# A decoder trunk in split float32: down projections of two ConvFFN parts from seven block products instead of eight

## The chip, the cores and the metric

The kernel runs on one core of a Trainium2 chip. The metric is the device time of one execution in microseconds. The time before is the median of three runs.

## The reference, cut to what matters

The trunk has two layers on 512 tokens with 1024 channels. Layer 0 mixes tokens with dilated attention, layer 1 with a Mamba-2 scan; each mixer is followed by a gated ConvFFN, and a last RMSNorm ends the trunk. The change is in the ConvFFN:

```python
def conv_ffn(h, w_up, conv_w, conv_b, w_down):
    u = causal_depthwise_conv(h @ w_up, conv_w, conv_b)
    gate, up = u[..., :D_FF], u[..., D_FF:]
    return (jax.nn.silu(gate) * up) @ w_down
...
for i in range(DEPTH):
    ...
    h = rmsnorm(x, ffn_norm_w[i])
    x = x + conv_ffn(h, ffn_w_up[i], ffn_conv_w[i], ffn_conv_b[i], ffn_w_down[i])
return rmsnorm(x, final_norm_w)
```

`D_FF` is 2816 and the convolution has three taps. All of it is float32.

## The kernel before, in words

**Layout.** Activations lie transposed: channels on the 128 partitions, the 512 tokens along the free axis. The residual stream is eight tiles `xr[0..7]` of 128x512. The normalised input of a projection is kept as eight pairs of tiles, `xh[k]` and `xl[k]`: a rounded high part and the remainder, both in the 4-byte type float32r.

**Split products.** A float32 product is built from three products of such parts: `mm3` (L136) issues high weights by high data, high weights by low data, low weights by high data, all added up in one PSUM bank. Each goes through `long_product` (L133 to L134), so nearly all of TensorE's matmuls carry line 134. One matmul has 128 rows of contraction, 128 output channels and 512 tokens.

**Weights.** `load_unit` (L116) fetches a block of 128x1024 float32 weights by one DMA on SyncE's queue into a tile `raw` (a ring of 4 buffers, `wr`), rounds it to `hi` on ScalarE (L125) and puts the remainder into `lo` on VectorE (L126). `hi` and `lo` have rings of 5 buffers each (`wh`), so the weights of at most five units exist at a time.

**ConvFFN.** `ffn` (L610) works through the 22 blocks of hidden channels in three parts of 8, 8 and 6 blocks (`FF_PARTS`). For each block `c` there are two up projections, gate and up (units `2c` and `2c+1`), each of 8 x 3 matmuls (`project`, L146) into a bank of the ring `mm` (3 banks). VectorE scales the bank by the row norms `rbc` into an SBUF tile `us` (L620), which frees the bank. `conv` then makes tile `a` from `us`: ScalarE applies the last tap and the bias (L603), VectorE adds the two other taps (L605). ScalarE applies Silu (L624), GpSimd multiplies gate and up (L627), ScalarE rounds the result to `g_h` (L629) and GpSimd makes `g_l` (L630). Then the part's down projection follows: `down` (L263) runs over the eight output blocks `m`, with one weight unit of up to 128x1024 each and 3 matmuls for each hidden block, and VectorE adds the finished bank to `xr[m]` (L640). In a part of 8 hidden blocks that is 8 x 8 x 3 = 192 matmuls. The last part of layer 1 goes through `finish` (L1059), which computes the last two output blocks in halves of 256 tokens: its matmuls have 256 columns, its residual adds (L1076) 256 too.

**Other buffers.** PSUM has three rings: `mm` with 3 banks, `aux` with 3 and `side` with 2. In SBUF, the ring `a` has 13 tiles of 128x512, `us` 3, `high` and `low` 8 each (the split activations of one part), `tmp` and `sq` 2 each. Tiles `xdt`, `yt`, `lm`, `ee` and `prev` belong to the scan of layer 1.

**Order.** A planner orders each engine's instructions by a simulated time line when the kernel is built. Where the code opens `manual_schedule` for TensorE, as around `down`, TensorE's order is that of the code, while VectorE, ScalarE and GpSimd are still ordered by the planner. The engines execute their queues strictly in order, and SyncE's queue issues the DMAs of weights.

## Time and profile before

| what | value |
|---|---|
| median of three runs | 1626.72 us (1626.13 to 1626.76) |
| the profiled execution's own time | 1626.55 us |
| its span, first to last instruction | 1624.6 us |
| mean granted TensorE clock | 0.999 |
| matmuls of one part of 8 hidden blocks | 192, at 588.2 to 630.4 us for the first |
| such parts | four: parts 0 and 1 of both layers |

In the profile, PE is TensorE's matmuls, PEld its weight loads, DVE VectorE, ACT ScalarE, POOL GpSimd and SP SyncE. A row of grouped instructions gives the line, the engine, the operation, the tiles written and read, the shapes and the count; then the busy time in us and the mean length of one in ns; then how long the engine stood idle just before, and what ended that. Matmuls are pipelined: a recorded length of 380 ns is not what one costs in a row of them, which is read from the distance between starts. The tiles of the down projections are named `wd` (and `wz` in `finish`), those of the up projections `u`.

### The profile page before, as it was taken

What the parts mean: (1) busy time and instruction counts of PE and PEld (TensorE: products, weight loads), DVE (VectorE), ACT (ScalarE), POOL (GpSimd) and SP (SyncE); (2) the same over time, 40 slices, a digit from 0 to 9 for tenths busy, and PEclk for the clock granted to TensorE, in tenths of its full rate; (3) what the DMA queues carried; (4) which work ended last, traced back from release to release, by engine and by line L of the source; (5) the groups of instructions that cost most, each with busy time, mean ns of one, the idle gap of its engine ahead of it and who ended that gap; (6) DMA issues with size and microseconds to landing.
All of it is one profiled execution on the core that took longest, in us unless ns stands there. A gap on an engine that the chain in (4) does not pass through costs nothing.

```text
span 1624.6 us, 21067 instructions
## 1 busy us (share of the span) xinstructions
PE 1615.7 (99%) x8038; PEld 1382.9 (85%) x8038; DVE 1082.8 (67%) x1813; ACT 655.0 (40%) x965; POOL 418.6 (26%) x272
## 2 busy tenths in 40 slices
PE   9999999999999999999999999999999999999998
PEld 8888888888888888888887888888888888888887
DVE  6366665266647855764657899988897784574564
ACT  5233332333334532432445455544443442342343
POOL 0444453045402320220231222222111341121020
PEclk9999999999999999999999999999999999999999
DMA  7322222222224323223233433334332232332321
GB/s 259 98 80 83 78 91 80 96 85 79 78 78 134 113 91 105 103 81 117 81 101 104 148 108 115 100 100 127 114 126 90 93 104 91 104 104 91 104 78 52
DMA packets 53235, 165.13 MB, mean 102 GB/s; under 512 B 6224, under 2 KB 9680, under 8 KB 53136
## 3 DMA queue, kind: packets, MB, share of 16 engines
q1 hardware_dynamic: 52304, 163.01, 30.5%
q8 instruction: 63, 1.03, 0.3%
q10 hardware_dynamic: 832, 0.79, 0.1%
q14 instruction: 36, 0.29, 0.1%
HBM read 161.62 MB, written 2.16 MB: 101 GB/s over the span
## 4 chain that ended last, share of the span: by engine, by line
PE 99%; ACT 0%; DVE 0%; POOL 0%; POOLq 0%; DVEq 0%; issue 0%
PE u L134 29%; PE qk L134 16%; PE wd L134 12%; PE v L134 8%; PE xs L134 5%; PE z L134 5%; PE wso L134 5%; PE wo L134 3%; PE c L134 3%; PE b L134 3%; PE wz L134 2%; PE py L830 1%; PE pg L490 1%; PE pp L477 1%; PE po L485 1%; PE pf L838 1%
## 5 line engine op out<-in xcount | busy, mean ns | idle before, releaser
L134 PE MATMUL u<-xh,lo_u 128*128 128x512 f32 x704 | 268.9, 382 | 0.0
L134 PE MATMUL u<-xh,hi_u 128*128 128x512 f32 x704 | 268.8, 382 | 0.0
L134 PE MATMUL u<-xl,hi_u 128*128 128x512 f32 x704 | 266.3, 378 | 0.0
L627 POOL TENSOR_TENSOR au<-au,au 128x512 f32<-128x512 f32 x43 | 58.5, 1360 | 422.2 <-DVE au L605 396.6
L605 DVE SCALAR_TENSOR_TENSOR au<-usu,par,au 128x511 f32<-128x511 f32 (+1 forms) x176 | 159.4, 911 | 7.6 <-ACT au L603 2.9
L125 ACT CAST hi_u<-raw_u 128x1024 fp32r<-128x1024 f32 x88 | 91.1, 1044 | 168.4 <-PE u L134 95.6
L388 POOL TENSOR_TENSOR rotqk<-rotqk,sr 32x512 f32<-32x512 f32 x48 | 88.2, 1837 | 250.2 <-DVE rotqk L387 239.8
L134 PEld LDWEIGHTS u<-xl,hi_u 128*128 128x128 f32 x704 | 131.7, 187 | 24.5
L134 PEld LDWEIGHTS u<-xh,lo_u 128*128 128x128 f32 x704 | 131.7, 187 | 24.0
L134 PEld LDWEIGHTS u<-xh,hi_u 128*128 128x128 f32 x704 | 131.7, 187 | 21.8 <-issue 0.4
L134 PE MATMUL qk<-xh,hi_qk 128*128 128x512 f32 x384 | 148.6, 387 | 0.0
L134 PE MATMUL qk<-xh,lo_qk 128*128 128x512 f32 x384 | 147.1, 383 | 0.0
L134 PE MATMUL qk<-xl,hi_qk 128*128 128x512 f32 x384 | 145.6, 379 | 0.0
L126 DVE TENSOR_TENSOR lo_u<-raw_u,hi_u 128x1024 fp32r<-128x1024 f32 x88 | 113.8, 1299 | 29.9 <-ACT hi_u L125 29.9
L620 DVE TENSOR_TENSOR usu<-u,rbc 128x512 f32<-128x512 f32 x88 | 60.3, 690 | 93.1 <-PE u L134 86.4
L640 DVE TENSOR_TENSOR xr<-xr,wd 128x512 f32<-128x512 f32 x40 | 27.3, 688 | 116.9 <-PE wd L134 116.9
L125 ACT CAST hi_qk<-raw_qk 128x1024 fp32r<-128x1024 f32 x48 | 50.3, 1047 | 130.3 <-PE qk L134 69.3
L134 PEld LDWEIGHTS qk<-xh,lo_qk 128*128 128x128 f32 x384 | 71.8, 187 | 13.3
L134 PEld LDWEIGHTS qk<-xl,hi_qk 128*128 128x128 f32 x384 | 71.9, 187 | 12.8
L389 POOL TENSOR_TENSOR qk<-qk,rotqk 32x512 f32<-32x512 f32 x48 | 81.5, 1698 | 3.8
L125 ACT CAST hi_wd<-raw_wd 128x1024 fp32r<-128x1024 f32 (+1 forms) x48 | 46.1, 972 | 88.7 <-PE wd L134 55.6
L134 PEld LDWEIGHTS qk<-xh,hi_qk 128*128 128x128 f32 x384 | 71.9, 187 | 11.2
(647 smaller groups left out, 3768.5 us busy)
## 6 DMA issues: line engine op xcount, KB each, us to landing
raw_u<-in_wup SPq DMA_DIRECT2D x88, 512.0 KB, 3.3
raw_qk<-in_wqk SPq DMA_DIRECT2D x48, 512.0 KB, 3.3
raw_wd<-in_wdn SPq DMA_DIRECT2D x32, 512.0 KB, 3.2
raw_xs<-in_win SPq DMA_DIRECT2D x16, 512.0 KB, 3.3
raw_z<-in_win SPq DMA_DIRECT2D x16, 512.0 KB, 3.4
lm<-rows SPq DMA_DIRECT2D x32, 256.0 KB, 5.4
raw_wso<-in_wso SPq DMA_DIRECT2D x16, 512.0 KB, 3.3
raw_v<-in_wv SPq DMA_DIRECT2D x12, 512.0 KB, 3.5
```

Of the source, the lines that this page charges most:

```text
L125: SC.copy(hi[:, s], raw[:, s])
L126: low.tensor_tensor(lo[:, s], raw[:, s], hi.bitcast(F32)[:, s], op=ALU.subtract)
L134: T.matmul(in_turns(dst), w, in_turns(x), start=first, stop=last)
L388: G.tensor_tensor(rot[R, :], rot[R, :], sr[R, :], op=ALU.mult)
L389: G.tensor_tensor(at(t)[R], at(t)[R], of(rot)[R], op=ALU.add)
L477: T.transpose(pp[:, b * P : (b + 1) * P], pr[:, b * P : (b + 1) * P], ident)
L485: T.matmul(po[:, ii], v0[h][:, b * P : (b + 1) * P], pts[i][:, (b - i + 1) * P : (b - i + 2) * P], start=b == max(i - 1, 0), stop=b == i,)
L490: T.matmul(pg[:, ii], vt[g, half][i][:, es], pts[i][:, (g + 1) * P : (g + 2) * P], start=g == 1, stop=g == 2,)
L605: V.scalar_tensor_tensor(dst[:, j:], src[:, : S - j], col(c_w + taps - 1 - j), dst[:, j:], op0=ALU.mult, op1=ALU.add,)
L620: V.tensor_tensor(us, p, rbc, op=ALU.mult)
L627: by.tensor_tensor(ab[1], ab[0], ab[1], op=ALU.mult)
L640: V.tensor_tensor(xr[m], xr[m], p, op=ALU.add)
```

## The change

Parts 0 and 1 of each ConvFFN no longer go through `down`. Hidden blocks are taken in pairs (2 by 2 blocks of weights for each pair of output blocks, 2 hidden blocks by 2 halves of 256 tokens of data), and the four output quarters are built from seven block products by Winograd's form of Strassen's algorithm.

- **Data sums.** For each pair of hidden blocks `c`, `c+1`, GpSimd forms four 256-column sums (`split_first`, `split_second`); ScalarE rounds them and GpSimd makes the remainders, as for the plain halves.
- **Weight sums.** `load_sevens` fetches the four 128x512 weight blocks of a pair of output blocks with four DMAs, forms four 128x512 sums on VectorE, and splits seven blocks of 128x512 (three tiles of 1024 columns and one of 512) on ScalarE and VectorE.
- **Products.** `down_by_sevens` runs over four pairs of output blocks. Each has seven groups of 4 hidden pairs x 3 matmuls with 256 columns, into four half banks (three of `aux`, one of `side`), TensorE in the code's order. Two banks are copied out half-way on ScalarE (`s1`, `s5`), and VectorE and GpSimd add the results to the two tiles of `xr`.
- **Order of the parts.** The first hidden block of the next part (`held`) is projected before the part's down projection.
- **Up projections.** VectorE scales the bank in place, and `conv` reads the bank instead of `us`.

Part 2 of each layer keeps `down` or `finish`. `mm3` and `long_product` only gain a flag that is passed through to the matmul. The weights' layout in HBM follows the new order of fetching.

```diff
@@ -607,45 +607,167 @@
                 op0=ALU.mult, op1=ALU.add,
             )
 
+    def gated(layer, c):
+
+        ab = []
+        for gu in range(2):
+            i = 2 * c + gu
+            n = f"u{layer}_{i}"
+            p = project(A["wup"][layer * 44 + i], n)
+            V.tensor_tensor(p, p, rbc, op=ALU.mult)
+            a = t2("a" + n, "a", 13, lp)
+            conv(a, p, C_FCW + (layer * 44 + i) * 3, C_FCB + layer * 44 + i, 3)
+            ab.append(a)
+        SC.activation(ab[0], ab[0], AF.Silu)
+
+        by = V if layer == 1 and c == NFF - 1 else G
+        by.tensor_tensor(ab[1], ab[0], ab[1], op=ALU.mult)
+        return ab[1], by
+
+    H0, H1 = slice(0, 256), slice(256, 512)
+
+    def split_by(by, high, low, src):
+        SC.copy(high, src)
+        by.tensor_tensor(low, src, high.bitcast(F32), op=ALU.subtract)
+
+    def split_whole(c, g, by):
+        h, l = high_low(f"g{c}")
+        split_by(by, h, l, g)
+        return h, l
+
+    def split_first(c, ga):
+
+        y = t2(f"y{c}", "a", 13, lp)
+        G.tensor_tensor(y[:, H0], ga[:, H1], ga[:, H0], op=ALU.subtract)
+        h, l = high_low(f"g{c}")
+        split_by(G, h[:, H0], l[:, H0], ga[:, H0])
+        split_by(G, h[:, H1], l[:, H1], y[:, H0])
+        return y, (h, l)
+
+    def split_second(c, ga, gb, y, j, fourth):
+
+        x = t2(f"x{c}", "a", 13, lp)
+        G.tensor_tensor(x[:, H0], gb[:, H1], y[:, H0], op=ALU.subtract)
+        G.tensor_tensor(y[:, H1], gb[:, H0], x[:, H0], op=ALU.subtract)
+        G.tensor_tensor(x[:, H1], gb[:, H1], ga[:, H1], op=ALU.subtract)
+        if j % 2 == 0:
+            fourth[:] = [
+                lp.tile([P, 512], F32R, tag="xdt", name=f"f{c}h", bufs=2),
+                lp.tile([P, 512], F32R, tag="yt", name=f"f{c}l", bufs=2),
+            ]
+        xhl = (
+            lp.tile([P, 512], F32R, tag="lm", name=f"x{c}h", bufs=4),
+            lp.tile([P, 512], F32R, tag=("ee", "prev")[j // 2], name=f"x{c}l", bufs=2),
+        )
+        half = slice(j % 2 * 256, j % 2 * 256 + 256)
+        f = tuple(t[:, half] for t in fourth)
+        split_by(G, xhl[0][:, H0], xhl[1][:, H0], x[:, H0])
+        split_by(G, *f, y[:, H1])
+        b = split_whole(c, gb, G)
+        split_by(G, xhl[0][:, H1], xhl[1][:, H1], x[:, H1])
+        return xhl, f, b
+
+    def load_sevens(src, name):
+
+        def raw(t):
+            return wr.tile([P, 1024], F32, tag="raw", name=f"raw{t}_{name}")
+
+        def split_weights(r, t):
+            n = r.shape[-1]
+            hi, lo = (wh.tile([P, 1088], F32R, tag=k, name=f"{k}{t}_{name}")[:, 0:n] for k in ("hi", "lo"))
+            split_by(V, hi, lo, r)
+            return hi, lo
+
+        a, b, c = (raw(t) for t in "abc")
+        q = t2(f"q_{name}", "a", 13, lp)
+        W0, W1 = slice(0, 512), slice(512, 1024)
+        dma(a[:, W0], src[:, 0:512])
+        dma(q, src[:, 512:1024])
+        dma(b[:, W1], src[:, 1024:1536])
+        dma(c[:, W0], src[:, 1536:2048])
+        V.tensor_tensor(a[:, W1], q, b[:, W1], op=ALU.add)
+        V.tensor_tensor(b[:, W0], a[:, W1], a[:, W0], op=ALU.subtract)
+        V.tensor_tensor(c[:, W1], c[:, W0], b[:, W0], op=ALU.subtract)
+        V.tensor_tensor(q, a[:, W0], q, op=ALU.subtract)
+        return [split_weights(r, t) for r, t in ((a, "a"), (b, "b"), (c, "c"), (q, "d"))]
+
+    def down_by_sevens(layer, part, pairs):
+
+        n = f"wd{layer}{part}"
+        for mp in range(KD // 2):
+            a, b, c, d = load_sevens(A["wds"][(layer * 2 + part) * 4 + mp], f"{n}{mp}")
+            r1, r3, r2, r4 = (
+                (side_bank if i == 1 else aux_bank)(f"{n}{mp}r{i}")[:, 0:256] for i in range(4)
+            )
+            top, low = xr[2 * mp], xr[2 * mp + 1]
+            kept_sums = t2("kept", "tmp", 2, lp)
+            sums = t2("sums", "sq", 2)
+            s1, s5, u, w = kept_sums[:, H0], kept_sums[:, H1], sums[:, H0], sums[:, H1]
+
+            def products(dst, weights, at, operand, begin):
+                for j, pair in enumerate(pairs):
+                    mm3(
+                        dst, *weights, at + j, *(t for t in operand(*pair)),
+                        begin and j == 0, j == len(pairs) - 1, skip=True,
+                    )
+
+            def halves(t, h):
+                return [x[:, h] for x in t]
+
+            products(r1, a, 0, lambda x, f, g0, g1: halves(g0, H0), True)
+            SC.copy(s1, r1)
+            products(r3, a, 4, lambda x, f, g0, g1: halves(g0, H1), True)
+            SC.copy(s5, r3)
+            products(r2, b, 0, lambda x, f, g0, g1: halves(x, H0), True)
+            V.tensor_tensor(u, s1, r2, op=ALU.add)
+            G.tensor_tensor(top[:, H1], top[:, H1], u, op=ALU.add)
+            products(r4, b, 4, lambda x, f, g0, g1: f, True)
+            V.tensor_tensor(low[:, H0], low[:, H0], r4, op=ALU.add)
+            products(r1, c, 0, lambda x, f, g0, g1: halves(g1, H0), False)
+            V.tensor_tensor(top[:, H0], top[:, H0], r1, op=ALU.add)
+            products(r3, c, 4, lambda x, f, g0, g1: halves(g1, H1), False)
+            V.tensor_tensor(top[:, H1], top[:, H1], r3, op=ALU.add)
+            G.tensor_tensor(low[:, H1], low[:, H1], s5, op=ALU.add)
+            products(r2, d, 0, lambda x, f, g0, g1: halves(x, H1), False)
+            V.tensor_tensor(w, s1, r2, op=ALU.add)
+            low3 = low.rearrange("p (h t) -> p h t", h=2)
+            V.tensor_tensor(low3, low3, w.unsqueeze(1).to_broadcast([P, 2, 256]), op=ALU.add)
+
     def ffn(layer, done):
+        held = None
         for part, (c0, cn) in enumerate(FF_PARTS):
-            gh, gl = [], []
+            gs = []
+            pairs, fourth = [], []
             for c in range(c0, c0 + cn):
-                ab = []
-                for gu in range(2):
-                    i = 2 * c + gu
-                    n = f"u{layer}_{i}"
-                    p = project(A["wup"][layer * 44 + i], n)
-                    us = t2("us" + n, "us", 3, lp)
-                    V.tensor_tensor(us, p, rbc, op=ALU.mult)
-                    a = t2("a" + n, "a", 13, lp)
-                    conv(a, us, C_FCW + (layer * 44 + i) * 3, C_FCB + layer * 44 + i, 3)
-                    ab.append(a)
-                SC.activation(ab[0], ab[0], AF.Silu)
-
-                by = V if layer == 1 and c == NFF - 1 else G
-                by.tensor_tensor(ab[1], ab[0], ab[1], op=ALU.mult)
-                g_h, g_l = high_low(f"g{c}")
-                SC.copy(g_h, ab[1])
-                by.tensor_tensor(g_l, ab[1], g_h.bitcast(F32), op=ALU.subtract)
-                gh.append(g_h)
-                gl.append(g_l)
+                g, by = held if c == c0 and held else gated(layer, c)
+                gs.append(g)
+                if part == len(FF_PARTS) - 1:
+                    pairs.append(split_whole(c, g, by))
+                elif c % 2 == 0:
+                    first = split_first(c, g)
+                else:
+                    y, g0 = first
+                    x, f, g1 = split_second(c, gs[-2], g, y, len(pairs), fourth)
+                    pairs.append((x, f, g0, g1))
+            if part < len(FF_PARTS) - 1:
+                held = gated(layer, c0 + cn)
+                with tc.manual_schedule(engines={mybir.EngineType.PE}):
+                    down_by_sevens(layer, part, pairs)
+                continue
             n = cn * P
 
             def load(m):
-                i = (layer * len(FF_PARTS) + part) * KD + m
-                return (*load_unit(A["wdn"][i][:, :n], f"wd{i}", n), 0)
+                return (*load_unit(A["wdn"][layer * KD + m][:, :n], f"wd{layer}{m}", n), 0)
 
             def add(m, p):
                 V.tensor_tensor(xr[m], xr[m], p, op=ALU.add)
-                if part == len(FF_PARTS) - 1:
-                    done(m)
-
-            if layer == 1 and part == len(FF_PARTS) - 1:
-                finish(load, lambda c: (gh[c], gl[c]), cn)
+                done(m)
+
+            if layer == 1:
+                finish(load, lambda c: pairs[c], cn)
                 return
             with tc.manual_schedule(engines={mybir.EngineType.PE}):
-                down(f"wd{layer}{part}", load, range(KD), lambda c: (gh[c], gl[c]), cn, add, late=True)
+                down(f"wd{layer}{part}", load, range(KD), lambda c: pairs[c], cn, add, late=True)
 
     def ups(layer, some):
         return [(A["wup"][layer * 44 + i], f"u{layer}_{i}") for i in some]
```

More of the change, by code (lines that the diff above doesn't have):

```diff
@@ L131, in in_turns, with long_product, mm3 @@
         return ap.rearrange("p (a b f) -> p b a f", b=4, f=4)
-    def long_product(dst, w, x, first, last):
-        T.matmul(in_turns(dst), w, in_turns(x), start=first, stop=last)
-    def mm3(dst, hi, lo, at, rh, rl, first, last):
+    def long_product(dst, w, x, first, last, skip=False):
+        T.matmul(in_turns(dst), w, in_turns(x), start=first, stop=last, skip_group_check=skip)
+    def mm3(dst, hi, lo, at, rh, rl, first, last, skip=False):
         w_h = hi[:, at * P : (at + 1) * P]
         w_l = lo[:, at * P : (at + 1) * P]
-        long_product(dst, w_h, rh, first, False)
-        long_product(dst, w_h, rl, False, False)
-        long_product(dst, w_l, rh, False, last)
+        long_product(dst, w_h, rh, first, False, skip)
+        long_product(dst, w_h, rl, False, False, skip)
+        long_product(dst, w_l, rh, False, last, skip)
     loaded = {}
@@ L1194, in _layout @@
     dn = a["ffn_w_down"].reshape(2, NFF, P, KD, P)
-    wdn = np.zeros((2, len(FF_PARTS), KD, P, 8, P), f)
-    for part, (c0, cn) in enumerate(FF_PARTS):
-        wdn[:, part, :, :, :cn] = dn[:, c0 : c0 + cn].transpose(0, 3, 2, 1, 4)
-    w["wdn"] = wdn.reshape(-1, P, 1024)
+    c0, cn = FF_PARTS[-1]
+    w["wdn"] = dn[:, c0 : c0 + cn].transpose(0, 3, 2, 1, 4).reshape(2 * KD, P, cn * P)
+    blocks = dn[:, :c0].reshape(2, 2, 4, 2, P, 4, 2, P)
+    w["wds"] = np.stack(
+        [blocks[:, :, :, k, :, :, m].transpose(0, 1, 4, 3, 2, 5) for m, k in ((0, 0), (1, 0), (1, 1), (0, 1))], axis=4
+    ).reshape(16, P, 2048)
     win = a["ssm_w_in"][0]
```

## The prediction, made before the result was known

> **What bounds the kernel now.** I read the page first: how busy each engine is, the clock, and the chain of work that ended last.
>
> ```profile
> span 1624.6 us, 21067 instructions
> PE 1615.7 (99%) x8038; PEld 1382.9 (85%) x8038; DVE 1082.8 (67%) x1813; ACT 655.0 (40%) x965; POOL 418.6 (26%) x272
> PEclk9999999999999999999999999999999999999999
> PE 99%; ACT 0%; DVE 0%; POOL 0%; POOLq 0%; DVEq 0%; issue 0%
> ```
>
> The chain is TensorE for 99% of the span, at full clock. Only fewer or shorter matmuls can shorten this kernel; work on any other engine costs nothing until TensorE waits for it. So I need the price of the removed matmuls, that of the added ones, and how full the other engines become in the changed stage. The table of windows gives the first, over the four stages that change (one row each, then the sum):
>
> ```profile
> 588.20:630.44 42.24, 42.24 (x193) 35.90 (x192) 15.07 (x17) 9.35 (x11) 2.57 (x2) 1.00 0.26 88
> 714.92:757.16 42.24, 42.24 (x193) 35.90 (x192) 15.06 (x17) 9.64 (x11) 2.57 (x2) 1.00 0.26 87
> 1349.82:1392.06 42.24, 42.24 (x194) 35.90 (x193) 15.07 (x17) 9.36 (x11) 2.57 (x2) 1.00 0.27 87
> 1476.54:1518.78 42.24, 42.24 (x194) 35.90 (x193) 15.08 (x17) 9.36 (x11) 2.57 (x2) 1.00 0.26 87
> sum 168.96, PE 168.96 PEld 143.62 DVE 60.27 ACT 37.71 POOL 10.28; mean PE 42.24 PEld 35.90 DVE 15.07 ACT 9.43 POOL 2.57
> ```
>
> The columns are the length, then busy time of PE, PEld, DVE, ACT and POOL (counts in brackets), clock, DMA share and GB/s. Each stage is 192 matmuls in 42.24 us, 0.220 us for each of 512 columns, without a gap. VectorE works 15.07 us of it, GpSimd 2.57: there is room, and DMA is at 26%. One execution takes 1626.55 us by its own time, 1.95 more than its span and 0.17 below the median of 1626.72, so the sum is made against 1626.55.
>
> **Part 1: the matmuls.** A pair of output blocks took 2 x 8 x 3 = 48 matmuls of 512 columns. Now it takes 7 groups x 4 x 3 = 84 of 256. Matmuls of that size, with the same kind of operands, stand at the kernel's end. Their recorded length, 0.27, hides their price; the starts show it (columns: start, length, engine):
>
> ```profile
> 1605.89 0.27 PE L134 MATMUL wz<-g16h,hi_wd 128*128 128x256 f32 x1
> 1606.00 0.27 PE L134 MATMUL wz<-g16l,hi_wd 128*128 128x256 f32 x1
> ...
> 1610.01 0.28 PE L134 MATMUL wz<-g16h,hi_wd 128*128 128x256 f32 x1
> ...
> 1612.91 0.36 PE L134 MATMUL wz<-g16h,hi_wd 128*128 128x256 f32 x1
> 1613.11 0.28 PE L134 MATMUL wz<-g16l,hi_wd 128*128 128x256 f32 x1
> 1613.23 0.28 PE L134 MATMUL wz<-g16h,lo_wd 128*128 128x256 f32 x1
> ```
>
> 36 of them start between 1605.89 and 1610.01, so 4.12 / 36 = 0.114 us each; single distances run from 0.11 to 0.12, and I take 0.115. Two halves cost 0.230 against 0.220 for a whole: of the eighth that the seven products save, a third goes to the shorter matmuls. A pair of output blocks costs 84 x 0.115 = 9.66 us, a part 38.64, all four parts 16 x 9.66 = 154.6. The saving is 168.96 - 154.6 = **14.4 us**. With 0.113 it would be 17.1, with 0.118 10.4; these are the bounds of this term.
>
> The Trainium skill, TensorE: Matmul & The Clock Gate, section "Back-to-back issue gap", gives an isolated matmul of N columns N / 2.4 + 2.5 ns, which for 256 is 109 ns, and says that in a stream of weight loads and matmuls both set the spacing. By the first, the 1344 would take 146.7 us. The trace has 114 on average, so it bears out the second.
>
> **Part 2: VectorE, which gets most of the added work.** Rows for each kind of it (mean length is the second number behind the bar):
>
> ```profile
> L126 DVE TENSOR_TENSOR lo_wd<-raw_wd,hi_wd 128x1024 fp32r<-128x1024 f32 x32 | 39.5, 1246 | 7.1 <-ACT hi_wd L125 7.1
> L126 DVE TENSOR_TENSOR lo_v<-raw_v,hi_v 128x512 fp32r<-128x512 f32 x8 | 5.3, 684 | 0.0
> L853 DVE TENSOR_TENSOR yt<-yt,usz 128x512 f32<-128x512 f32 x16 | 10.5, 684 | 0.0
> L1076 DVE TENSOR_TENSOR xr<-xr,wz 128x256 f32<-128x256 f32 x4 | 1.7, 420 | 3.7 <-PE wz L134 3.7
> L605 DVE SCALAR_TENSOR_TENSOR au<-usu,par,au 128x511 f32<-128x511 f32 x88 | 92.4, 1052 | 4.9 <-ACT au L603 2.9
> L620 DVE TENSOR_TENSOR usu<-u,rbc 128x512 f32<-128x512 f32 x88 | 60.3, 690 | 93.1 <-PE u L134 86.4
> L849 DVE SCALAR_TENSOR_TENSOR yt<-axs,par,py 128x512 f32<-128x512 f32 x16 | 11.4, 742 | 0.5 <-PE py L830 0.3
> ```
>
> For each pair of output blocks: four weight sums of 512 at 0.684 (2.74), three remainders of 1024 at 1.246 (3.74) and one of 512 (0.68), 7.16 us for weights; then five 256-column operations on the half banks at 0.42 (2.10) and the last add over 512 columns (0.68), 2.78 for results. Together **9.94 us of VectorE against 9.66 us of TensorE**. So VectorE is the engine to watch: it went from a third of this stage to all of it.
>
> Whether TensorE waits depends on what VectorE has done ahead. The rings of `hi` and `lo` hold five tiles and a pair of output blocks uses four, so its weights can be made one pair, 9.66 us, ahead; the first pair's are made under the up projections before. Inside a part's 38.64 us VectorE must then do: the last up projection's scaling and taps (0.69 + 2 x 0.742 = 2.17), three pairs' weights (21.48), four pairs' results (11.12) and the first weight unit of the next up projections (1.25), 36.0 in all. It fits with 2.6 us to spare. The banks leave room as well: `r1` is added to `xr` two groups, 24 x 0.115 = 2.8 us, before the next pair needs its bank, `r4` later still, `r3` alternates between two banks, and the half-way copies have three groups, 4.1 us.
>
> ScalarE has 3.5 casts and two copies for each pair:
>
> ```profile
> L125 ACT CAST hi_wd<-raw_wd 128x1024 fp32r<-128x1024 f32 x32 | 33.0, 1043 | 74.3 <-PE wd L134 49.7 <-PE u L134 24.6
> L1065 ACT ACTIVATE xw<-xr,par 128x256 f32<-128x256 f32 x4 | 2.0, 494 | 0.0
> L316 ACT ACTIVATE v<-v,rcol 128x512 f32<-128x512 f32 x16 | 10.7, 689 | 7.7 <-PE v L134 5.3 <-POOL rcol L253 2.3
> ```
>
> That is 3.65 + 0.99 = 4.6 of 9.66 us: covered. The weights are as many bytes as before in four DMAs for two; the queue was at 88 GB/s, and the ring of four `raw` tiles lets it run ahead. I cost it at nothing; if it were late, VectorE's sums would be, which the rivals price.
>
> **Part 3: GpSimd's data sums.** The rows nearest to its 256-column work, those of its 512, and, first, two matmuls of the up projections:
>
> ```profile
> 587.76 0.38 PE L134 MATMUL u<-xl,hi_u 128*128 128x512 f32 x1
> 587.98 0.38 PE L134 MATMUL u<-xh,lo_u 128*128 128x512 f32 x1
> L1096 POOL TENSOR_TENSOR ot<-xw,rbc x3: 727/728/732, 1615.6 to 1617.0; 128x256 f32<-128x256 f32 x3
> L627 POOL TENSOR_TENSOR au<-au,au 128x512 f32<-128x512 f32 x43 | 58.5, 1360 | 422.2 <-DVE au L605 396.6 <-ACT au L624 13.8 <-issue 5.8
> L630 POOL TENSOR_TENSOR g9l<-au,g9h 128x512 fp32r<-128x512 f32 x2 | 3.6, 1802 | 3.2 <-ACT g9h L629 3.2
> ```
>
> Each pair of hidden blocks costs two multiplications (2.72), nine operations on 256 columns (6.57) and one remainder on 512 (1.80): 11.1 us under four up projections, whose matmuls also start 0.22 apart: 96 x 0.220 = 21.1 us. Covered. The critical place is the part's start, where the last pair's sums must be ready. Its chain from the last up bank: scaling 0.69, last tap 0.69, two taps 1.48, multiplication 1.36, three sums 2.19, the first remainder 0.73, which makes 7.1 us; the fourth operand 7.9, the plain block 9.7, the last remainder 10.4. TensorE meanwhile has the two projections that were moved ahead, 48 x 0.220 = 10.56 us, and first needs the third group's operand after two groups more, at 13.3. Six us of cover; without the moved projections the start would wait. I cost it at nothing.
>
> **Part 4: scaling in the bank.** Up projections start 0.220 us apart today, so there is no stall to win: 0 us. VectorE saves some, since the taps from a bank should cost 0.742 (the row that reads a bank, `py`) instead of 1.052. The price is a bank held for 2.9 us instead of 0.7; two other banks of `mm` cover 2 x 5.28 us. After a norm, three or four banks are scaled late; four units at 2.2 us each are 8.7 us, and TensorE meets the fourth bank after 13. Cost nothing; if a queue in front of it took 5 us more, at two norms, up to 10 us.
>
> **Sum.** 1626.55 - 14.4 = 1612.2. TensorE also loses a little where a stream breaks: the break at 1612.91 cost 0.20 instead of 0.115. For 16 pairs and four entries that is 20 x 0.085 = 1.7. **Forecast: 1614 us.**
>
> **Rivals.**
>
> *VectorE is late by its waits for ScalarE.* Each remainder waits for its cast: in the row above, 7.1 us over 32, or 0.22 each, 0.9 for each pair. The part's 36.0 becomes 39.6, 1.0 over TensorE's time, and the time 1612.2 + 3.8 = 1616. With some blocking by GpSimd it goes up to 1623. For it: VectorE has almost no slack. Against: it can work a pair ahead.
>
> *GpSimd blocks VectorE.* The range of the remainders in the list by line (min / median / max in ns):
>
> ```profile
> L126 DVE TENSOR_TENSOR lo_u<-raw_u,hi_u x88: 1210/1226/2301, 493.5 to 1556.8; 128x1024 fp32r<-128x1024 f32 x88
> ```
>
> Some take 1.1 us more than the usual 1.226, about a GpSimd operation. The two GpSimd adds of each pair of output blocks could each hold VectorE for their whole 0.73: 1.46 for each pair, 41.9 us for a part, 1.5 us saved in all: 1625, no change. The Trainium skill, SBUF — State Buffer, section "Who interferes with whom", states this rule: a VectorE operation with two SBUF inputs and a GpSimd operation that reads SBUF exclude each other, and whichever is second blocks fully. The long remainders agree with it. It speaks against the weight sums, and for taps that read a bank.
>
> *Slower: VectorE becomes the bound.* Both together, 2.36 for each pair, make 36.0 + 9.4 = 45.4 us for a part, 3.2 more than today: 1626.55 + 12.6 = 1639. The point from which it decides is 9.94 + (42.24 - 36.0) / 4 = 11.5 us of VectorE for a pair; below that the change still gains.
>
> *Shorter matmuls cost only 0.109,* as the closest starts have it (1605.89 and 1606.00). Then 1344 take 146.5 us, 22.5 are saved: 1604. Against it: the mean of 36.
>
> *The change does less than it says:* were a 256-column matmul at 0.126, 1344 would take 169 us and nothing would be gained. No stretch of the rows shows more than 0.12 without a break; I put this with no change.
>
> **How the numbers follow.** Forecast (1609.5 to 1616, the bounds of part 1 around it) 0.58; VectorE late by its waits (1616 to 1623) 0.22; no change 0.09; slower 0.07; cheaper matmuls 0.04. The range 1609 to 1623 holds the first two, 0.80. About 0.2%, or 3.3 us, is what a measurement of this kernel can tell from no change, so faster means below 1623.4: 0.58 + 0.22 + 0.04 = 0.84; same 0.09; slower 0.07.
>
> **What would show each step.** Matmuls of `wd` in the changed parts 0.113 to 0.118 us apart, a part in about 39 us; VectorE busy for over 90% of those stretches, with waits of TensorE for `lo` tiles or banks under 1 us for each part; GpSimd's last remainders done before the third group; up projections still 0.220 apart; taps near 0.75. I am wrong if the parts take 42 us or more: then look for what TensorE waits for, `lo` from VectorE in the later pairs, a bank of `aux` at a pair's start, or the sums of the last hidden pair at the entry.

## The result and the profile after

| kernel | median | profiled execution | its span | clock |
|---|---|---|---|---|
| before | 1626.74 us | 1626.55 us | 1624.6 us | 0.999 |
| after | 1665.24 us | 1664.71 us | 1662.9 us | 0.988 |

The changed kernel is slower: ratio 1.0237, 95% interval 1.022 to 1.0255. The forecast was 1614, with 0.80 on 1609 to 1623 and 0.07 on slower; the result is 51 us away and on the other side. Medians and ratios, here and below, leave out one run of e11 (3169.8 us) and one of the kernel before (2213.4), which ran at a lower clock. The page of the kernel after, first lines and the chain:

```profile
span 1662.9 us, 22788 instructions
PE 1615.8 (97%) x8614; PEld 1403.5 (84%) x8614; DVE 1147.6 (69%) x1973; ACT 713.0 (43%) x1093; POOL 553.5 (33%) x432
PEclk9999999999999989999999999999999999999999
PE 92%; DVE 4%; DMA 1%; issue 1%; ACT 1%; POOL 0%; SPq 0%; DVEq 0%; POOLq 0%; ACTq 0%
```

The kernel before had TensorE on the chain for 99%; now 8% of 1663 us belong to others (a share that is no measure of the loss: in e14 below, which is faster than the kernel before, TensorE has 82%), and the clock falls in places. VectorE is busy for 69% of the span, and in the changed parts, as the table of windows below shows, for 42.8 us of 49.4: nearer to full, but with room. The view of waits, for TensorE in the kernel after, names the places (total in us, times, longest):

```profile
PE u L134 <- DVE au L605: 5.3, 1, 5.3
PE wd010r L134 <- ACT hia_wd L630: 4.9, 1, 4.9
PE wd110r L134 <- ACT hia_wd L630: 4.9, 1, 4.9
PE wd000r L134 <- ACT hia_wd L630: 4.9, 1, 4.9
PE wd100r L134 <- ACT hia_wd L630: 4.9, 1, 4.9
PE wd100r L134 <- DVE loa_wd L631: 2.8, 1, 2.8
PE u L134 <- ACT au L621: 2.8, 1, 2.8
PE wd000r L134 <- DVE loa_wd L631: 2.7, 1, 2.7
PE wd010r L134 <- DVE loa_wd L631: 2.2, 1, 2.2
PE wd110r L134 <- DVE loa_wd L631: 2.1, 1, 2.1
```

Eight of the ten are at the entry of a changed part (the digits of `wd000r` are layer, part, pair of output blocks): TensorE waits for the first pair's weights, first the high parts, then the remainders. The other two are in the up projections, just behind the two norms. Together 37.5 us; the same view of the kernel before has no wait of `u` or `wd`. The windows of the four parts, each from its last up-projection matmul on (columns as in the prediction):

```profile
601.77:652.73 50.96, 42.78 (x338) 41.73 (x337) 42.93 (x61) 23.08 (x31) 15.53 (x12) 0.90 0.36 107
...
1518.87:1567.54 48.67, 41.61 (x338) 40.79 (x337) 42.07 (x61) 23.01 (x30) 16.14 (x10) 0.93 0.37 112
sum 197.53, PE 167.34 PEld 163.86 DVE 171.20 ACT 92.06 POOL 65.47; mean PE 41.84 PEld 40.96 DVE 42.80 ACT 23.01 POOL 16.37
```

Some 49 us for a part instead of 42.24, at a clock of 0.90 to 0.93. Why the weights are late stands in VectorE's timeline ahead of the first part (start, length; in brackets the idle time before, and what ended it), behind the row of SyncE that fetched the tiles `q` of the part's four pairs:

```profile
578.77 3.87 SPq L685 DMA_DIRECT2D q_wd<-in_wds  x4
...
596.91 0.70 DVE L617 TENSOR_TENSOR u<-u,rbc 128x512 f32<-128x512 f32 x1 [2.13 <-PE u L134]
598.52 1.54 DVE L605 SCALAR_TENSOR_TENSOR au<-u,par,au 128x511 f32<-128x511 f32 x2 [0.92 <-ACT au L603]
602.19 0.70 DVE L617 TENSOR_TENSOR u<-u,rbc 128x512 f32<-128x512 f32 x1 [2.13 <-PE u L134]
603.80 1.53 DVE L605 SCALAR_TENSOR_TENSOR au<-u,par,au 128x511 f32<-128x511 f32 x2 [0.91 <-ACT au L603]
605.25 0.68 DVE L688 TENSOR_TENSOR rawa_wd<-q_wd,rawb_wd 128x512 f32<-128x512 f32 x1
605.97 1.64 DVE L689 TENSOR_TENSOR rawb_wd<-rawa_wd 128x512 f32<-128x512 f32 x1
607.53 1.22 DVE L691 TENSOR_TENSOR q_wd<-rawa_wd,q_wd 128x512 f32<-128x512 f32 x1
```

The first `q` was fetched at 578.77; these four fetches took 3.0 to 3.7 us to land. VectorE then stood idle for 2.13 + 0.92 us in each up projection of 5.28. Yet the first sum (L688) runs at 605.25, behind the taps of the last moved projection, since VectorE's queue has it there: its inputs had lain ready for some 20 us. TensorE had issued its last up-projection matmul at 601.77. The other kind of wait, behind layer 1's norm, first TensorE and then VectorE:

```profile
1309.19 0.38 PE L134 MATMUL u<-xh,lo_u 128*128 128x512 f32 x1
1314.84 0.77 PE L134 MATMUL u<-xh,hi_u 128*128 128x512 f32 x1 [5.27 <-DVE au L605]
1315.40 0.63 PE L134 MATMUL u<-xl,hi_u 128*128 128x512 f32 x1
1315.83 0.63 PE L134 MATMUL u<-xh,lo_u 128*128 128x512 f32 x1
```

```profile
1308.51 3.08 DVE L617 TENSOR_TENSOR u<-u,rbc 128x512 f32<-128x512 f32 x5
1311.50 0.74 DVE L605 SCALAR_TENSOR_TENSOR au<-u,par,au 128x511 f32<-128x511 f32 x1
1312.16 1.21 DVE L126 TENSOR_TENSOR lo_u<-raw_u,hi_u 128x1024 fp32r<-128x1024 f32 x1
1313.29 2.05 DVE L605 SCALAR_TENSOR_TENSOR au<-u,par,au 128x511 f32<-128x511 f32 x3
```

Five scalings follow each other, so five banks are full when the norm comes. Scaling them no longer frees them; the taps do, and these stand behind five scalings and a remainder.

Below, TensorE's time is the distance from one matmul's start to the next, summed over the up projections (u) and the four changed parts:

| kernel | u | parts |
|---|---|---|
| before | 465.7 | 169.0 |
| after | 497.0 | 176.4 |

Together 38.8 us more, against 38.3 of the span; everything else differs by 0.4. The four waits for `hia` stand in u, because they follow an up projection's matmul.

### The profile page after: what moved, and what is told of

Read it like the earlier page. It is cut to its first block, busy times and chain, and to the rows that moved or that the text cites. A ratio compares the mean times of both kernels' runs of the same rounds, so it can differ in the third digit from the quotient of the medians.

```text
span 1662.9 us, 22788 instructions
## 1 busy us (share of the span) xinstructions
PE 1615.8 (97%) x8614; PEld 1403.5 (84%) x8614; DVE 1147.6 (69%) x1973; ACT 713.0 (43%) x1093; POOL 553.5 (33%) x432
## 4 chain that ended last, share of the span: by engine, by line
PE 92%; DVE 4%; DMA 1%; issue 1%; ACT 1%; POOL 0%; SPq 0%; DVEq 0%; POOLq 0%; ACTq 0%
PE u L134 27%; PE qk L134 15%; PE v L134 8%; PE xs L134 5%; PE z L134 5%; PE wso L134 5%; PE wo L134 3%; PE c L134 3%; PE b L134 3%; PE wz L134 2%; PE wd L134 2%; DMA rawb_wd<-in_wds 1%; PE py L952 1%; PE pg L490 1%; PE pp L477 1%
## 5 line engine op out<-in xcount | busy, mean ns | idle before, releaser
L605 DVE SCALAR_TENSOR_TENSOR au<-u,par,au 128x511 f32<-128x511 f32 (+1 forms) x176 | 130.4, 747 | 34.8 <-ACT au L603 30.9
L617 DVE TENSOR_TENSOR u<-u,rbc 128x512 f32<-128x512 f32 x88 | 60.9, 698 | 133.9 <-PE u L134 127.2
L126 DVE TENSOR_TENSOR lo_u<-raw_u,hi_u 128x1024 fp32r<-128x1024 f32 x88 | 113.8, 1295 | 34.8 <-ACT hi_u L125 34.7
L897 POOL TENSOR_TENSOR xdd<-xdt,dec 128x384 f32<-128x384 f32 x16 | 18.0, 1139 | 241.1 <-DVE xdt L896 241.1
L384 DVE TENSOR_TENSOR qk<-qk,cr 128x512 f32<-128x512 f32 x48 | 33.0, 688 | 72.7 <-PE qk L134 72.5
L126 DVE TENSOR_TENSOR lo_qk<-raw_qk,hi_qk 128x1024 fp32r<-128x1024 f32 x48 | 60.9, 1269 | 32.0 <-ACT hi_qk L125 32.0
```

The lines of the kernel that those rows point to most:

```text
L126: low.tensor_tensor(lo[:, s], raw[:, s], hi.bitcast(F32)[:, s], op=ALU.subtract)
L384: V.tensor_tensor(at(t), of(p), of(cr), op=ALU.mult)
L605: V.scalar_tensor_tensor(dst[:, j:], src[:, : S - j], col(c_w + taps - 1 - j), dst[:, j:], op0=ALU.mult, op1=ALU.add,)
L617: V.tensor_tensor(p, p, rbc, op=ALU.mult)
L897: G.tensor_tensor(v4(u[:, 0:384], 3), v4(t[:, 0:384], 3), b3(dec3[:, 0:3, heads[x]], 64), op=ALU.mult)
```

## The experiments

Two theories. **A, placement:** the first pair's sums stand too late in VectorE's queue because `q` lies in the ring `a`; its fetch waits until GpSimd releases a tile of that ring, and the planner orders VectorE by that time. The first half stands in the view of waits of SyncE's queue, between 573 and 590 us (L685 fetches `q`):

```profile
SPq L685 <- POOL g5l L631: 1.2, 1, 1.2
SPq L685 <- POOL x5l L631: 1.0, 1, 1.0
```

**B, banks:** scaling in the bank holds the banks behind a norm. The rival of both is that VectorE has too much work. Line numbers shift by one in kernels with the copy `us`. Each run stands beside runs of the kernel before on the same chip (medians 1626.0 to 1626.8).

**Copies back (e1).** Undoes part 4 alone.

```diff
-            V.tensor_tensor(p, p, rbc, op=ALU.mult)
+            us = t2("us" + n, "us", 3, lp)
+            V.tensor_tensor(us, p, rbc, op=ALU.mult)
...
-            conv(a, p, C_FCW + ...)
+            conv(a, us, C_FCW + ...)
```

> The changed kernel with the up projections scaled into SBUF tiles again; the rest of the change stays. Theory A (the first pair's weight sums stand too late in VectorE's queue, at the entry of each of the four parts) and theory B (banks held until the taps are done make TensorE wait after two norms, about 10 us of waits and slow clock): the two waits among the first up projections of each layer go, the four entries stay: 1655. Rival to B (those waits come from the longer queues of GpSimd and ScalarE for the data sums): they stay, 1665.

1658.17 us, ratio 1.0197 (1.018 to 1.0214), 3 us above the expected 1655. No wait behind a norm is left; the entries stay, and those of each layer's first part are longer (7.8, 5.4, 9.7 and 5.4 us between two starts, where the kernel after has 5.3).

**`q` in a spare buffer (e2).** One line; the program is otherwise the same.

```diff
-        q = t2(f"q_{name}", "a", 13, lp)
+        q = t2(f"q_{name}", ("btok", "cb")[int(name[-1]) % 2], 1, lp)
```

> The changed kernel with one edit: the fourth weight block q is fetched into one of two tiles of the scan that stand unused in the ConvFFN, instead of a tile of the ring a, whose previous user GpSimd releases late. Scaling in the banks stays. Theory A: the sums move ahead of the last up projections in VectorE's queue, the four entries of about 8 us each vanish, some 32 us: 1633, with the two waits after the norms left. Rival (VectorE is simply too full in these stages): the waits move into the later pairs of each part and the time stays over 1650.

1633.61 us, ratio 1.0044 (1.0029 to 1.0059); u 477.6, parts 165.6. The same windows of this kernel, summed:

```profile
sum 166.45, PE 161.00 PEld 156.72 DVE 139.07 ACT 84.62 POOL 81.55; mean PE 40.25 PEld 39.18 DVE 34.77 ACT 21.16 POOL 20.39
```

The four entries are gone. That the buffer decides is shown, with 31.6 us in all; that the planner went by the time of GpSimd's release is argued from the fetch and the order. VectorE has 34.8 us of work in a part of 41.6. The 31.6 is a balance: the four entries and first pairs give back 38.3 us, and the other pairs take 7.3 more than in the kernel after. There TensorE now waits for results that VectorE adds late, most of all in the second pairs, such as

```profile
PE wd001r L134 <- DVE xr L727: 0.9, 1, 0.9
```

So VectorE's load is felt too, at some 7 us and not at the 50 that were lost.

**Scaling in the bank alone (e3).** The kernel before, with only part 4:

```diff
-                    us = t2("us" + n, "us", 3, lp)
-                    V.tensor_tensor(us, p, rbc, op=ALU.mult)
+                    V.tensor_tensor(p, p, rbc, op=ALU.mult)
```

> The kernel before with one edit: up projections are scaled in their banks; down projections as before. Theory B: waits after the two norms as in the changed kernel, 5 to 10 us: 1632 to 1637. Rival (the waits come from the queues of the data sums): no new wait, 1627.

1635.26 us, ratio 1.0053 (1.0038 to 1.0068); u 474.7, so 9.0 us more than before, with distances of 0.97 and 5.65 us behind the two norms and matmuls 0.43 us apart behind the second. The view of waits:

```profile
PE u L134 <- DVE au L605: 5.9, 2, 5.3
```

B is shown: there are no data sums in this kernel. In layer 1 the wait is as long as in the kernel after; in layer 0, where that has 3.14 us, the data sums come on top.

**Both undone (e4).** Edits of e1 and e2 together.

> Both edits: up projections scaled into SBUF tiles again, and q in the scan's spare tiles. Theories A and B together: only the products' own saving is left, 1613 to 1616, faster than both kernels. Rival (VectorE too full): 1640 or more, with waits of TensorE for low parts in the second to fourth pair of each part.

1644.18 us, ratio 1.0109 (1.0093 to 1.0124): a miss by 28 us. u 472.6, parts 180.7. TensorE now waits in the first pair for the last hidden pair's data (`x7l` from GpSimd, 3.4 us idle), and the first pairs take 17.1, 12.2, 14.8 and 12.3 us. The first taps in the list by line of e2 and then of e4, both between 530 and 601 us (behind the bar: busy us, mean ns):

```profile
L605 DVE SCALAR_TENSOR_TENSOR au<-u,par,au 128x511 f32<-128x511 f32 x14 | 10.4, 747 | 3.7 <-ACT au L603 3.5
```

```profile
L605 DVE SCALAR_TENSOR_TENSOR au<-usu,par,au 128x511 f32<-128x511 f32 x14 | 13.1, 949 | 6.4 <-ACT au L603 6.3
```

With copies in SBUF the taps grow from 747 to 949 ns, and GpSimd's four kinds of data sums together from 14.4 to 17.1 us in this stretch, three of them longer and one shorter. That they hold each other up is argued from this, not shown apart. The two edits do not add up: the copies end the waits behind the norms and make the entries late.

**Sums written first (e5).** `q` stays in `a`; the fetches and four sums of a part's first pair are written ahead of the moved projection.

```diff
+                begun = sevens_of(layer, part, 0)
                 held = gated(layer, c0 + cn)
...
+            _, split_all = begun if mp == 0 else sevens_of(layer, part, mp)
```

> The changed kernel with only VectorE's order at the entry of a part touched: the fetches and the four sums of the first pair of output blocks are written ahead of the moved up projection, q stays in the ring a. The sums then stand between the scaling and the taps of the first moved projection, about 8 us earlier, and their remainders before the scaling of the last. Theory A (the place in VectorE's queue makes the entry late, not the fetch of q nor the buffer as such): entries shrink from 8 us to 2 or less, 1636 to 1644. Rival (on the chip q's fetch is late as well): 1660 or more.

1647.75 us, ratio 1.013 (1.0115 to 1.0145), 4 us above the range. The entries shrink to 0.9 to 1.5 us, and the same wait, for `loa`, appears in the second pair (3.6, 3.3, 2.7 and 3.3 us), whose `q` still lies in `a`. This agrees with A for the first pair. In the second the fetch itself is late, since `q` is fetched only at 607.93 and VectorE waits for it:

```profile
612.08 0.69 DVE L688 TENSOR_TENSOR rawa_wd<-q_wd,rawb_wd 128x512 f32<-128x512 f32 x1 [1.24 <-DMA q_wd<-in_wds]
```

**Copies for two hidden blocks behind each norm (e6), also with `r1` in a projection bank (e7), and e6 without the moved projection (e8).** These and all later variants have `q` in the spare buffer.

```diff
+            us = t2("us" + n, "us", 3, lp) if c < 2 else p
...
-                (side_bank if i == 1 else aux_bank)(f"{n}{mp}r{i}")[:, 0:256] for i in range(4)
+                (mm_bank, side_bank, aux_bank, aux_bank)[i](f"{n}{mp}r{i}")[:, 0:256] for i in range(4)
...
-                held = gated(layer, c0 + cn)
```

> The kernel with q in the scan's spare tiles, and in addition the first four up projections of each layer (the first two hidden blocks) scaled into SBUF tiles, all others in their banks. Theory B (a bank held until its taps are done costs only where the norm comes late): the 12 us that the up projections lost there go, and the cheaper taps elsewhere stay: 1621 to 1623. Rival (what e4 lost came with scaling into SBUF in whatever place): no gain, 1633 or more.

> e6 with the first result r1 of each pair in a bank of mm (idle in these stages), so that r2 and r4 alternate between three aux banks. The waits left in e6 are at the start of the second to fourth pair, for a bank whose result VectorE has not yet added. If the bank's place is the cause: about 8 of the 11 us that the products take over 154.6 go, 1612 to 1616. Rival (VectorE full): the waits move on to low parts, 1620 or more.

> e6 without the projection that was moved ahead of each part's products. The recorded step says that the last hidden pair's sums are ready 7 us after the last up bank and that the third group of products needs them after 2.8 us: a wait of 4 to 6 us for each part, 16 to 24 us over e6: 1638 to 1646. If the products never waited for GpSimd, it would be as e6.

e6: 1637.61 us, ratio 1.0065 (1.0048 to 1.0082); e7: 1635.21, 1.0052 (1.0037 to 1.0067). Both miss. The waits behind the norms moved to the first blocks that scale in their bank, and in layer 1 grew from 5.65 to 6.85 us (u 478.3 and 477.7). The bank for `r1` took 2.4 us off the parts. e8: 1686.06, ratio 1.0364 (1.0349 to 1.038), 48 us over e6 where 16 to 24 were expected: the distances in which TensorE waits for the last hidden pair's `x` tiles (`x7h` and `x7l` in parts 0) are 8.75 and 3.73 us in each part, twice to three times what was expected. The cover of the moved projection is needed.

**More of the same (e9 to e12).** e9 writes the split of hidden block 0 behind the gating of block 1 (bank scaling throughout). e10 is e7 with `c < 8`. e11 is e6 with `c < 5` and e9's edit. e12 has copies throughout, `r1` in a projection bank, and two hidden blocks gated ahead of a part's products:

```diff
+                for c in (c0 + cn, c0 + cn + 1):
+                    held[c] = gated(layer, c)
```

> As the variant with q in a spare buffer (1633.61 us), with one step more: the split of hidden block 0 of each layer is written behind the gating of hidden block 1, so that ScalarE's first tap of the next up projection (line 603) is queued ahead of the cast of g0 (line 630). In the trace of the spare-buffer variant VectorE sat idle for 3.19 us at 535.09 for that tap, and the tap stood behind a cast that waited 1.40 us for GpSimd's gate product. Theory 'ScalarE's order behind a norm holds the banks': the TensorE wait of 3.15 us in layer 0 goes, with the halved clock behind it (about 1 us); the wait of 5.65 us in layer 1 stays, since there five scalings of 3.08 us stand in front of the taps: 1629 to 1631. Rival 'VectorE has too much to do behind a norm, whatever the order': 1633 to 1635.

> Spare buffer for q, r1 in a projection bank, and the scaled copy in SBUF for all eight hidden blocks of each layer's first part (16 up projections), the scaling in the bank for the rest. Theory 'banks are short only while the backlog behind a norm lasts': the two waits of the up projections (2.65 and 6.85 us in the variant with two hidden blocks) go and move nowhere, u falls from 478.3 to 466-468 us, and the pairs stay near 166: 1622 to 1625. Rival 'taps that read SBUF beside GpSimd's sums are slower and come late at the entry, as in the variant with copies for all blocks': the first part's first pair grows by 4 to 7 us per layer, 1630 to 1638.

> Spare buffer for q, the scaled copy for the first five hidden blocks of each layer, the scaling in the bank for the rest, and the split of hidden block 0 written behind the gating of hidden block 1. Theory 'banks are short only while the backlog behind a norm lasts': no wait of the up projections is left, u near 467 and pairs 166 to 168: 1622 to 1626, which would be within 0.2% of the kernel before or better. Rival 'the wait moves to whichever block scales in its bank first, as it did with two blocks': a TensorE wait of 2 to 7 us at the sixth hidden block of each layer, 1632 to 1638.

> Scaled copies in SBUF for all hidden blocks, q in a spare buffer, r1 in a projection bank, and two hidden blocks of the next part gated before a part's products instead of one, so that the chain of the last hidden pair's sums lies under 21.1 us of up projections instead of 10.6. Theory 'the chain at the entry has too little cover': the entries of 17.1, 12.2, 14.8 and 12.3 us (variant with copies and spare buffer) fall to about 10.5, 16 us less, and with r1 in a projection bank 2 us more: 1626 to 1628, about the kernel before. Rival 'the whole stage is late, since taps and GpSimd's sums slow each other': the second block only puts more taps and banks in the queue, entries stay over 12 us or the up projections wait: 1636 to 1645.

| kernel | median, ratio | u | parts |
|---|---|---|---|
| e9 | 1633.74, 1.0045 (1.003 to 1.006) | 476.1 | 166.1 |
| e10 | 1634.88, 1.0054 (1.0038 to 1.007) | 471.6 | 171.5 |
| e11 | 1637.00, 1.0063 (1.0045 to 1.0081) | 473.5 | 172.2 |
| e12 | 1635.92, 1.0058 (1.0041 to 1.0075) | 475.9 | 168.4 |

All four times are those of the rival (e12's lies 0.1 us below its range). Its mechanism holds in e10, whose first pairs in part 0 grow to 16.7 and 14.0 us. e9's 3.15 us became 0.97 and 1.22 us. e11's waits are not at the sixth hidden block but at the seventh to ninth and at the entries. In all the waits go from the up projections to a part's entry, or back, at about the same total: u and parts together are 642 to 647 us in e2, e6, e7 and these four. More copies and more cover were not what lacked.

**Without the data sums (e13).** As e4, but GpSimd's four sums and differences for each pair of hidden blocks are left out, and the plain blocks are split in their place.

```diff
-        G.tensor_tensor(y[:, H0], ga[:, H1], ga[:, H0], op=ALU.subtract)
...
-        G.tensor_tensor(x[:, H0], gb[:, H1], y[:, H0], op=ALU.subtract)
-        G.tensor_tensor(y[:, H1], gb[:, H0], x[:, H0], op=ALU.subtract)
-        G.tensor_tensor(x[:, H1], gb[:, H1], ga[:, H1], op=ALU.subtract)
```

> As the variant with scaled copies for all hidden blocks and q in a spare buffer (1644.18 us), but the four sums and differences of the gated products (lines 641 and 650 to 652) are left out and the blocks themselves split in their place; all casts, remainders, products and weight sums stay. GpSimd loses 4 operations of 0.74 to 1.6 us per pair of hidden blocks. Theory 'GpSimd's data sums and the chain through them make the taps and the entries late': entries fall to 10-11 us and the up projections' waits go: 1618 to 1624. Rival 'VectorE and ScalarE are late by their own load': less than 8 us is gained, 1636 or more.

1631.04 us, ratio 1.0027 (1.0016 to 1.0039), between the two theories: 13 us less than e4. u 466.3: no wait behind a norm is left. The parts keep 173.5; the largest single excess is one first pair of 16.55 us, where TensorE waits 3.7 us for a copy on ScalarE; what delays that copy stays open. So with the copies the sums do make the up projections late, by 6.3 us of u; whether by amount or place, the next pair tells.

**The data sums two to three blocks later (e14, e15).** All work is done. In each layer's first part the splits run behind their blocks by a table; `r1` in a projection bank, `q` spare; e14 has copies for three blocks, e15 none.

```diff
+                upto = {0: 0, 1: 0, 2: 0, 3: 2, 4: 2, 5: 4, 6: 5, 7: 8}[c - c0] if part == 0 else c - c0 + 1
+                while nsplit[part] < upto:
...
+            us = t2("us" + n, "us", 3, lp) if c < 3 else p
```

> Spare buffer for q, r1 in a projection bank, scaled copies for the first three hidden blocks of each layer, and GpSimd's data sums of the first part written two to three hidden blocks later, so that the stretch behind a norm has none of them. If their place behind the norm is what makes the banks wait: the up projections' waits go (u 466 to 468 us, from 478), the pairs stay near 166 or rise by 2 to 4 us at the first part's entry: 1620 to 1626, the first version at or below the kernel before. If their amount is: the waits come back at the later blocks or at the entry, 1630 to 1636.

> The same with the scaling in the bank throughout. In the kernel before with the scaling in the bank alone, the up projections lost 9.0 us without any data sums, so if the banks wait by themselves about 9 us are lost here too: u 474 to 476, 1628 to 1633; if it is the sums' place alone, 1620 to 1626.

e14: **1623.11 us, ratio 0.9978 (0.9969 to 0.9988): 0.2% faster than the kernel before,** a small difference, but clear of the interval. u 466.2, as before the change; parts 165.8 against 169.0. e15: 1630.71, ratio 1.0027 (1.0017 to 1.0037), u 474.1. The first line of the page of e14, and its longest waits of TensorE:

```profile
span 1621.7 us, 22755 instructions
```

```profile
PE wd100r L134 <- POOL x7l L632: 1.7, 1, 1.7
...
PE wd112r L134 <- DVE sums L723: 0.8, 1, 0.8
...
PE wd000r L134 <- POOL f5l L632: 0.7, 1, 0.7
PE wd100r L134 <- POOL f5l L632: 0.7, 1, 0.7
```

None of the waits behind a norm is left, and the amount of the sums is not what makes u long: e14 makes all of them and has u as in e13, which has none. With the sums at once u stayed between 471.6 and 478.3, with copies for no, two, five, eight or all hidden blocks; with the sums later and three blocks copied it is 466.2. Three blocks with the sums at once were not run, so the two edits' shares are not told apart there. Without copies, later sums bring 3.5 us of u (e2 to e15, which also moves `r1`): layer 0's wait falls to the 0.97 us of e3, and layer 1's stays at 5.65. And the banks cost by themselves: e15 differs from e14 by the copies alone and has 7.9 us more in u.

## Why the prediction was wrong, point by point

- **Part 1 was right.** Undisturbed pairs take 9.63 to 9.65 us in the kernel after, 84 x 0.1147; the forecast had 9.66. The matmuls do save 14.4 us.
- **Part 2 had the price right and the place wrong.** Taps from the bank take 747 ns on the page of the kernel after (0.742 in the forecast), and VectorE's 36.0 us for a part came out as 34.8 in e2 (in the kernel after it is 42.8, with the first pair's weights inside). The row with 1.052 that was set beside it is only the first of the two taps that VectorE adds to each up projection; both together have a mean of 0.911. **The step that failed** is "the first pair's are made under the up projections before". There was room, but the queue had the sums behind the last taps. The waits at the four entries cost 4 x 5.30 us between starts for the high parts and 3.10 + 2.61 + 3.23 + 2.56 for the remainders, 32.7, less 1.3 of usual distance: 31.4. With the slow clock behind them it is 40.6: 20.3 ahead of the first product, and 58.8 for the four first pairs instead of 38.5. That e2's 31.6 is so near to 31.4 is chance, since it is what was left of the larger sum after the new waits in its second and third pairs. The sign to look for was a part of 42 us or more, and it came, but the list behind it had the later pairs' `lo` and not the first pair's weights. The forecast read durations and ring sizes, and not in whose ring `q` lies, who frees it, or what that does to the order.
- **Part 4 failed as "Cost nothing".** Its own other end, "up to 10 us" at two norms, was the one: 9.0 alone (e3), 7.9 between e15 and e14. Four units "at 2.2 us each" was wrong because the scalings are not interleaved with the taps: five come first (3.08 us at 1308.51), and no bank is freed by them.
- **Part 3 held on the average and failed in one place.** 11.1 us of GpSimd under 21.1 is covered, except behind a norm, where the up projections' own chain has a backlog. Starting the sums there cost 3.5 us of u without copies (e2 against e15) and 6.3 with copies for all blocks (e4 against e13, which leaves the sums out); e7 (477.7) is 11.5 over e14, but differs in the number of copied blocks too. The chain at the entry was sized right: in the kernel after, GpSimd's last remainder of the part starts at 601.01 and takes 0.73 us, and TensorE's last moved matmul starts at 601.77. That the moved projection is needed at the entry was right (e8).
- **The rivals.** The result lies on the side of the slower one, but not by its mechanism: it asked for a VectorE that is full, and VectorE idled 3 us in each up projection ahead of the entry. Operations do grow beside GpSimd's (e4), but that did not decide the time of the kernel after, as e2 has the same GpSimd work.
- **The sum, mended.** 1614 + 31.4 (waits at the entries) + 11.1 (the rest of u: two waits of 8.4 and 2.7 of slow clock) + 9.0 gives 1665.5, against 1664.71 for the profiled execution. The 9.0 is what the pairs take over the forecast besides the waits: 176.35 - 154.6 - 11.04 waiting for remainders = 10.7, of which 1.7 was in the sum. Nearly all lies in the first pairs, where the clock is halved.

Open stay the 11.2 us that e14's parts take over 154.6 (its waits name GpSimd's remainders of the last hidden pair and VectorE's `sums`), why the wait in layer 1 grew in e6, e13's first pair, and the shares of the copies and of the later sums in e14.

## What to carry to other kernels

Room on an engine is not yet a place in its queue: for each added operation ask which buffer its inputs and outputs are taken from, who frees that buffer, and so behind what the in-order queue will have it. A step that ends the early freeing of a PSUM bank is paid behind a norm, where several banks are full at once, and not in the steady state where it is looked at. When a change saves 14 us and loses 53, undo its parts one at a time: three edits of placement and three copied blocks, with all of the work kept, turned +2.4% into -0.2%.

## What the runs showed of the hardware that was not expected

**A wait costs more than its length.** After 5.27 us of idleness at 1314.84 TensorE's matmuls of 512 columns start 0.43 us apart instead of 0.22, for the next ten or so, and the window 1314.8 to 1319.3 has a granted clock of 0.50. At the entries it is those of 256 columns, in the kernel after:

```profile
607.07 0.58 PE L134 MATMUL wd000r<-g0h,hia_wd 128*128 128x256 f32 x1 [4.92 <-ACT hia_wd L630]
607.44 0.42 PE L134 MATMUL wd000r<-g0l,hia_wd 128*128 128x256 f32 x1
610.54 0.58 PE L134 MATMUL wd000r<-g0h,loa_wd 128*128 128x256 f32 x1 [2.68 <-DVE loa_wd L631]
610.92 0.42 PE L134 MATMUL wd000r<-g2h,hia_wd 128*128 128x256 f32 x1
611.13 0.41 PE L134 MATMUL wd000r<-g2l,hia_wd 128*128 128x256 f32 x1
```

They start 0.21 apart where 0.115 is usual. The Trainium skill, TensorE: Matmul & The Clock Gate, section "Part 1: The HAM clock gate (the "warmup" mystery)", says that after an idle window of about 3.4 us TensorE's clock is halved, and is full again after about as long a stretch of work. The traces agree for the long waits: each of 4.9 us or more was followed by slow matmuls, and the slow stretches lasted 3 to 6 us. For shorter ones they show no such limit. After the wait with 2.76 us of idleness behind layer 0's norm in the kernel after, the distances are 0.22 again from the second matmul on; after the same wait in e2 they are not:

```profile
538.03 0.76 PE L134 MATMUL u<-xh,hi_u 128*128 128x512 f32 x1 [2.77 <-ACT au L621]
538.60 0.63 PE L134 MATMUL u<-xl,hi_u 128*128 128x512 f32 x1
539.02 0.63 PE L134 MATMUL u<-xh,lo_u 128*128 128x512 f32 x1
```

Six distances of 0.43 us follow there, and in e12 even a wait of 1.93 us is followed by eight. So the same wait can cost some 1.5 us more in one kernel than in another.

**Taps from a bank were shorter than taps from SBUF.** VectorE's two taps of an up projection together, in the kernel before and then in the kernel after:

```profile
L605 DVE SCALAR_TENSOR_TENSOR au<-usu,par,au 128x511 f32<-128x511 f32 (+1 forms) x176 | 159.4, 911 | 7.6 <-ACT au L603 2.9
L605 DVE SCALAR_TENSOR_TENSOR au<-u,par,au 128x511 f32<-128x511 f32 (+1 forms) x176 | 130.4, 747 | 34.8 <-ACT au L603 30.9
```

Between 530 and 601 us the two take 949 and 964 ns from the SBUF copies of e4, and 747 and 746 from the banks of e2. The forecast had held the rule of the Trainium skill, SBUF — State Buffer, section "Who interferes with whom", against the weight sums. The trace agrees there: the first of them, at 605.25, takes 0.68 us, and the next, at 605.97, takes 1.64 and ends 0.55 us behind a GpSimd product that runs from 605.47 to 607.06.
